# Sums of weight blocks by accumulating transfers in place of VectorE, with two signs turned and P4 last in each pair

## The chip, the core and the metric

The kernel runs on one core of a Trainium2 chip. The core has a matrix engine (TensorE, PE in the profile, with PEld for its weight loads), a vector engine (VectorE, DVE), an activation engine (ScalarE, ACT), a general engine (GpSimd, POOL) and a queue that only issues transfers (SyncE, SP). Each engine works through its own list of instructions in order, and waits for the others by semaphores. Transfers (DMAs) run beside the engines on 16 DMA engines that all queues share. The metric is the time of one execution on the device, in microseconds.

## The reference

One decoder block on 1024 tokens of width 1024, all in float32:

```
proj = x @ w_in                     # 1024 x 7168: q, f, i, og, pool_v, gate_a, gate_b
a = HGRN2(silu(q), f, i)            # 8 heads of 128, a gated recurrence in time
a = rmsnorm(a) * g * sigmoid(og) @ w_a
b = w_pool . (causal mean of pool_v over 2, 4, 8, 16 tokens - pool_v) * pool_scale
mix = (sigmoid(gate_a) * a + sigmoid(gate_b) * b) @ w_out
x = LN(alpha * x + mix)
x = LN(alpha * x + relu(x @ w_up)^2 @ w_down)
```

The products are most of the work: with w_in, w_a, w_out, w_up (1024 x 4096) and w_down (4096 x 1024).

## The kernel before

**Precision.** A float32 operand is split into a high part in the type that TensorE multiplies (a copy on ScalarE, `A.copy`, L118) and a low part, the rest (a subtraction on VectorE, L119). A product is then three matmuls, high x high, high x low and low x high.

**The half-size scheme.** All large products but the one with w_out use Strassen's scheme in the form that Winograd gave it: both operands are cut into 2 x 2 blocks, and seven products of half size replace eight. The activations' blocks (a11, a12, a22) and sums (s1 to s4) are made once per stage, split and kept (`xp`). The weights' sums are made anew for every pair of column blocks. A pair is two blocks of 128 columns, each cut into an upper and a lower half of the rows: b11 and b21 are the first block's halves, b12 and b22 the second's, each 128 partitions x 512 values (256 KB). Its seven products, each 12 matmuls of 128 x 128 by 128 x 512 (four row blocks, three matmuls each), are

| product | activation | weights | adds to |
|---|---|---|---|
| P1 | a11 | b11 | bank a |
| P2 | a12 | b21 | bank c |
| P7 | s3 | b22 - b12 (t3) | bank z |
| P6 | s2 | t3 + b11 (t2) | bank a |
| P4 | a22 | b21 - t2 (t4) | bank z |
| P5 | s1 | b12 - b11 (t1) | bank a |
| P3 | s4 | b22 | bank a |

A bank is a region of PSUM, the memory that TensorE writes. Between P1, P6, P5 and P3, which add onto the same bank, its running value is taken out: P1's and P6's by a copy on ScalarE (L271), P5's by an addition on VectorE (L275). P7's value is copied from bank z before P4 adds to it.

**`pair`** (L263) builds these steps: `t3`, `t2`, `t4`, `t1` make the weights' sums on VectorE (`w_diff`, L241; L284; L289) into a tile of the ring t (two buffers), and `w_part` splits a block or a sum into two tiles of the ring w (ten buffers, so five operands at a time). `p1` to `p7` are the products with what takes their results. With `twin=True` two pairs run interleaved and have an order of their own. `run` (L357) issues the steps of one pair, or of several together.

**Loads.** A pair's four blocks come by SP into two buffers of the ring raw: one holds b11 and b12, the other b21 and b22. For neighbouring column blocks a half is one transfer of 512 KB (L217), otherwise each block is one of 256 KB (L223).

**Stages.** (1) The values i of all heads, by rows of tokens. (2) The heads: for each of eight heads the pair of its q and f columns (`head_inputs`), and for two halves of the tokens the recurrence (`hgrn`), in which VectorE, ScalarE, GpSimd (small products of decays: T, eq and ek, L819 to L838) and TensorE take turns; between them stand the pairs of the output gates, of the pooling and, towards the end, of the gates (`gates`, `pool_products`). (3) The product with w_a, in twin pairs. (4) The product with w_out and the first norm. (5) The pairs of w_up: the first two as twins, the third with its blocks in other buffers, thirteen more alone (L1211), each followed by the sums of its squared ReLUs that the next stage needs. (6) w_down and the second norm.

**The order.** The kernel is written with a framework that plans the order on each engine from a simulated timeline: it takes the ready instruction that the program has first, changed by `high_priority` and `issue_after`. What the program writes pair after pair is therefore interleaved with neighbouring pairs and with the recurrence. In the program a pair's order is P1, P2, then P6 and P7, then P5 and P4, then P3. The order in which each queue then runs is fixed.

GpSimd issues eight transfers in this kernel (`load_y`, L1293, rows of the residual stream of 4 KB each); all others come from SP, and a few from ScalarE.

Of the kernel before, what the change touches and what calls it, by code (L numbers as in the profile page):

```python
# [43 lines left out]
def tile_hybrid_block(  # L44
# [126 lines left out]

    def first_tokens(name, *tags):
        for kp in range(CH):
            ps, _ = transposed(r[:CH], HALF if name == "a12" else 0, kp, tags[kp % len(tags)])
            in_parts(name, kp, ps)
            A.copy(xt[name == "a12"][kp], ps)

    def second_tokens(name, *tags):
        a11, a12, s = xt
        turned = []  # L180
        for kp in range(CH):
            if name in ("s3", "a22"):
                ps, done = transposed(r[CH:], HALF if name == "a22" else 0, kp, tags[kp % len(tags)])
                turned.append(done)
            if name == "s3":
                V.tensor_sub(s[kp], a11[kp], ps)
            elif name == "s1":
                V.tensor_add(a11[kp], s[kp], a11[kp])
            elif name == "s4":
                V.tensor_sub(a12[kp], a12[kp], s[kp])  # L190
            in_parts(name, kp, dict(s3=s, s2=s, s1=a11, s4=a12)[name][kp] if name != "a22" else ps)
            if name == "a22":
                V.tensor_sub(s[kp], ps, s[kp])
        return turned
# [44 lines left out]
    def w_diff(a, b):  # L239
        t = wq.tile([P, CH, P], F32, tag="t", name=nm("t"), bufs=2)  # L240
        V.tensor_sub(t, a, b)  # L241
        return t

# [19 lines left out]
    def pair(raw, rooms, takes, pz_tag="pj", twin=False, pc_tag="pj"):  # L263


        b11, b12, b21, b22 = raw if len(raw) == 4 else (raw[kh][:, :, n] for kh in range(2) for n in range(2))
# [11 lines left out]
        def t3():  # L278
            c["t"] = w_diff(b22, b12)
            return w_part(c["t"])  # L280

        def t2():
            if not twin:
                V.tensor_add(c["t"], c["t"], b11)  # L284
            return w_part(c["t"])

        def t4():
            if not twin:
                V.tensor_sub(c["t"], b21, c["t"])  # L289
                return w_part(c["t"])  # L290
            V.tensor_add(c["t"], c["t"], b11)
            V.tensor_sub(b21, b21, c["t"])
            return w_part(b21)

        def t1():
            return w_part(w_diff(b12, b11))
# [46 lines left out]
        def b_22():  # L343
# [8 lines left out]
                else (((t3, t2), ((t2, p6), (t3, p7))), ((t1, t4), ((t1, p5), (t4, p4))))  # L352
            ),
            ((b_22,), ((b_22, p3),)),
        )
# [46 lines left out]
    with tc.tile_pool(name="xr", bufs=8, side="right", reuse_waits="tile") as xr:  # L402
# [122 lines left out]
        def take_p5(c, ps):  # L525
            V.tensor_add(c22[c], c22[c], ps)
            put(1, 1, c, c22[c])

        def take_p3(c, ps):
            t = c_soon()  # L530
            A.copy(t, ps)
            put(0, 1, c, t)
# [9 lines left out]
        with behind_parts("a12"):  # L542
            for k in range(CH):
                V.tensor_sub(b22[k], b22[k], b12[k])
            w = parts(b22)
# [3 lines left out]
        with behind_parts("s3"):  # L549
            for k in range(CH):  # L550
                V.tensor_add(b22[k], b22[k], b11[k])
                V.tensor_sub(b21[k], b21[k], b22[k])
            w = parts(b21)
# [7 lines left out]
        with tc.issue_after(taken["a22", 1]):  # L561
            for k in range(CH):
                V.tensor_sub(b12[k], b12[k], b11[k])
            w = parts(b12)
# [40 lines left out]
    def o_sums(kp, tile_of=c_tile):  # L605

        a11, a21, a12, a22 = (loaded(od[k][u], tile_of) for k, u in ((kp, 0), (kp, 1), (kp + CH, 0), (kp + CH, 1)))
        V.tensor_add(a22, a21, a22)
        V.tensor_sub(a21, a11, a21)
        V.tensor_sub(a11, a22, a11)  # L610
        V.tensor_sub(a12, a12, a11)
        for name, t in zip(("s3", "s2", "s1", "s4"), (a21, a11, a22, a12)):
            nc.sync.dma_start(out=osd[name][kp], in_=t)
# [4 lines left out]
    with tc.tile_pool(name="tmp", bufs=1, side="right", reuse_waits="tile") as tmp:  # L618
# [24 lines left out]
        def head_inputs(h, behind=()):  # L643
# [6 lines left out]
            def take_f(u):  # L650
                def take(src):
                    t = fs[u] = fs[u] or tt("f")
                    A.activation(t, src, AF.Sigmoid)
                    A.activation(t, t, AF.Identity, bias=lb[:, h : h + 1], scale=one_lb[:, h : h + 1])
                return take

            def take_q(u):
# [7 lines left out]
                loaded_blocks(w_in, h * P, D + h * P), (c_soon, c_late, room_f),  # L665
# [8 lines left out]
        def output_gates(h):  # L674

            def take(dst, src=False):
                def put(t):
                    s = c_late() if src else t
                    A.activation(s, t, AF.Sigmoid)
                    nc.sync.dma_start(out=dst, in_=s)  # L680
                return put

            run(pair(
                loaded_blocks(w_in, 3 * D + h * P, 3 * D + (h + 1) * P), (c_soon, c_late, c_late),
                (take(ogd[h][0]), take(ogd[h + 1][0], True), take(ogd[h][1]), take(ogd[h + 1][1])),
            ))

        def gates(j):
# [3 lines left out]
            def take(dst, src=None, more=None):  # L692
                def put(t):
                    s = (tt("v") if spare else c_late()) if src else t
                    more_of = loaded(more, lambda: tt("v")) if more is not None else None
                    A.activation(s, t, AF.Sigmoid)
# [7 lines left out]
                loaded_blocks(w_in, 5 * D + j * P, 6 * D + j * P), rooms,  # L704
                (take(gad[j][0]), take(gbd[j][0], True, more[0]), take(gad[j][1]), take(gbd[j][1], False, more[1])),
# [26 lines left out]
        def pooled(g):  # L732
# [3 lines left out]
            def mean(c, u):  # L736

                for lo in (QUARTER, 0):
# [8 lines left out]
                    if u == 0 and lo == 0:  # L747
                        n += win - 1
                        V.tensor_mul(cur[:, HALO:n], cur[:, HALO:n], inv_n[:, : win - 1])
                        V.tensor_sub(pv[:, HALO:n], cur[:, HALO:n], pv[:, HALO:n])  # L750
                    V.scalar_tensor_tensor(pv[:, n:], cur[:, n:], 1.0 / win, pv[:, n:], ALU.mult, ALU.subtract)
# [11 lines left out]
            def first(c, i):  # L763
                G.memset(c[:, :HALO], 0.0)
                mean(c, 0)
                put(c, i, 0)

            def second(c, i):
                mean(c, 1)
# [12 lines left out]
            def take_12(ps):  # L782
# [7 lines left out]
                loaded_blocks(w_in, 4 * D + j * P, 4 * D + (j + 1) * P),  # L790
# [154 lines left out]
        nxt = head_inputs(0, (None, None, "p6", None, None))  # L945
# [40 lines left out]
        def gated(j, u, park):  # L986

            def take(src):
                t = loaded(gad[j][u], mg_tile("ga", 12))
                V.tensor_mul(t, t, src)  # L990
# [10 lines left out]
        def a_pair(p):  # L1001
            raw = loaded_blocks(w_a, 2 * p * P, (2 * p + 1) * P, raw_tile if p % 2 else mg_raw)
            room = mg_tile("room", 4)
            takes = [gated(2 * p + i, u, p < 2) for u in range(2) for i in range(2)]
# [131 lines left out]
    with tc.tile_pool(name="up", bufs=1, side="right", reuse_waits="tile") as up:  # L1136
# [10 lines left out]
        def relu2(t, src):  # L1147
            A.activation(t, src, AF.Relu)
# [3 lines left out]
        def units(i, raw):  # L1152
# [5 lines left out]
            def take(n):  # L1158
                def take(src):
                    h[n] = relu2(c_tile() if n == 1 else src, src)  # L1160
                return take

            def last(src):
                take(1)(src)
                h11, h12, h21, h22 = h
# [15 lines left out]
            return pair(raw, (c_tile,) * 3, (take(0), last, take(2), take(3)), "hg", i < 2, "tr" if i == 2 else "pj")  # L1181
# [29 lines left out]
        for i in range(3, NP):  # L1211
            raw, load = up_blocks(i)
            w_load = load(0, 1)
            if i == NP - 2:
                for part in down_rows(0, ws0):
                    part(w_load)
# [185 lines left out]
```

## Time and profile before

| | |
|---|---|
| median of 3 runs | 1461.77 us (1460.99 to 1465.17) |
| the profiled execution | 1460.19 us, span 1458.5 us |
| TensorE busy | 1436.4 us |
| VectorE busy | 1141.6 us |
| ScalarE busy | 758.3 us |
| GpSimd busy | 58.6 us |
| moved by DMA | 226.82 MB |

The profile is of one execution. The page gives the busy time of each engine, the same in 40 equal slices of the span with the clock that was granted to TensorE (PEclk) and the busy share of the DMA engines, then the chain of work that ended last, and groups of instructions by line. In a group, `out<-in` are the program's names, then the shapes, `xcount | busy, mean ns of one | idle time before them <- what ended it`. A row of waits reads: engine, what it wanted to write and its line, `<-` what it waited for: us in total, times, longest. A row of DMA issues ends with the size in KB and the median us from issue to landing. A row of stretches gives their length and, for each engine, busy us and the number of instructions, then the granted clock, the DMA share and GB/s. A timeline row is start, duration, engine, line, operation. `L118` is line 118.

### The profile page before, as it was taken

The page shows a single profiled execution, that of the slowest core. Times are in us where ns is not written, and L with a number is a line of the kernel's source. Part 1 is how long each engine was busy: PE and PEld are TensorE (multiplying, and loading weights), DVE is VectorE, ACT ScalarE, POOL GpSimd, SP SyncE. Part 2 cuts the span into 40 slices and gives each one's busy share as a digit, 9 for nine tenths or more (in the row PEclk, how much of TensorE's full clock was granted, in tenths as well). Part 3 has the DMA queues.
Part 4 walks back from the last instruction along what each step waited for, and adds up shares of the span by engine and source line. Part 5 has one row for each costly group of instructions (what it writes and reads, how often), then busy time and mean ns, then how long its engine had stood idle before and what let it go on. Part 6 is the DMA issues. An engine that isn't in the chain of part 4 may idle for free.

```text
span 1458.5 us, 20662 instructions
## 1 busy us (share of the span) xinstructions
PE 1436.4 (98%) x7377; PEld 1187.9 (81%) x7377; DVE 1141.6 (78%) x1838; ACT 758.3 (52%) x1383; POOL 58.6 (4%) x244
## 2 busy tenths in 40 slices
PE   8999999999999998999999999999999999999997
PEld 7888888888888886788888878888888888888886
DVE  5967989899898885768985597666666787777977
ACT  5445565666656655556542376555555443333535
POOL 0001001001000010000002100000000100000000
PEclk9999999999999999999999999999999999999999
DMA  7232233323234447897672225444474874445322
GB/s 253 70 126 87 85 98 101 109 75 114 90 99 138 152 132 249 301 299 241 223 247 99 73 94 195 159 146 144 152 261 149 275 260 150 153 141 163 130 73 116
DMA packets 160615, 226.82 MB, mean 156 GB/s; under 512 B 11232, under 2 KB 84480, under 8 KB 160512
## 3 DMA queue, kind: packets, MB, share of 16 engines
q1 hardware_dynamic: 158576, 218.93, 44.7%
q0 software_dynamic: 1152, 4.19, 0.8%
q10 hardware_dynamic: 784, 2.38, 0.5%
q8 instruction: 58, 0.95, 0.3%
q14 instruction: 45, 0.37, 0.1%
HBM read 154.16 MB, written 71.30 MB: 155 GB/s over the span
## 4 chain that ended last, share of the span: by engine, by line
PE 94%; DVE 3%; DMA 1%; ACT 1%; issue 0%; SPq 0%; DVEq 0%
PE ps_pj L201 16%; PE ps_pj L203 16%; PE ps_pj L204 16%; PE ps_pj L1283 4%; PE ps_pj L1285 4%; PE ps_pj L1284 4%; PE ps_pj L106 3%; PE ps_pj L107 3%; PE ps_pj L105 2%; PE ps_tr L1285 1%; PE ps_tr L1283 1%; PE ps_tr L1284 1%; PE ps_sc L201 1%; PE ps_sc L203 1%; PE ps_sc L204 1%; PE ps_hg L203 1%
## 5 line engine op out<-in xcount | busy, mean ns | idle before, releaser
L201 PE MATMUL ps_pj<-act,w 128*128 128x512 f32 x1068 | 421.6, 395 | 0.4 <-ACT act L123 0.2
L203 PE MATMUL ps_pj<-act,w 128*128 128x512 f32 x1068 | 415.1, 390 | 0.5 <-DVE act L124 0.5
L204 PE MATMUL ps_pj<-act,w 128*128 128x512 f32 x1068 | 414.1, 390 | 0.0
L201 PEld LDWEIGHTS ps_pj<-act,w 128*128 128x128 f32 x1068 | 200.6, 188 | 42.8 <-ACT act L123 0.6
L204 PEld LDWEIGHTS ps_pj<-act,w 128*128 128x128 f32 x1068 | 200.5, 188 | 42.3
L203 PEld LDWEIGHTS ps_pj<-act,w 128*128 128x128 f32 x1068 | 200.6, 188 | 40.6 <-DVE act L124 0.9
L118 ACT CAST w<-t 128x512 fp32r<-128x512 f32 x170 | 104.7, 620 | 105.0 <-PE ps_pj L203 53.8
L118 ACT CAST w<-raw 128x512 fp32r<-128x512 f32 x143 | 88.2, 620 | 117.3 <-PE ps_pj L203 62.5
L119 DVE TENSOR_TENSOR w<-raw,w 128x512 fp32r<-128x512 f32 x143 | 99.8, 702 | 55.2 <-ACT w L118 53.9
L119 DVE TENSOR_TENSOR w<-t,w 128x512 fp32r<-128x512 f32 x170 | 115.9, 685 | 29.6 <-ACT w L118 29.4
L1245 ACT CAST act<-act 128x1024 fp32r<-128x1024 f32 x66 | 66.9, 1050 | 107.9 <-issue 35.0
L1246 DVE TENSOR_TENSOR act<-act,act 128x1024 fp32r<-128x1024 f32 x66 | 79.3, 1220 | 18.5 <-ACT act L1245 15.8
L1285 PE MATMUL ps_pj<-act,act 128*128 128x512 f32 x240 | 92.9, 389 | 0.0
L1284 PE MATMUL ps_pj<-act,act 128*128 128x512 f32 x240 | 92.9, 389 | 0.0
L1283 PE MATMUL ps_pj<-act,act 128*128 128x512 f32 x240 | 92.4, 389 | 0.0
L275 DVE TENSOR_TENSOR c<-c,ps_pj 128x512 f32<-128x512 f32 x95 | 64.5, 681 | 18.0 <-PE ps_pj L204 13.4
L271 ACT COPY c<-ps_pj 128x512 f32<-128x512 f32 x96 | 55.2, 582 | 12.8 <-PE ps_pj L204 12.8
L817 DVE RECIPROCAL tC<-tA 128x128 f32<-128x128 f32 x64 | 54.1, 904 | 0.0
L1284 PEld LDWEIGHTS ps_pj<-act,act 128*128 128x128 f32 x240 | 45.1, 188 | 9.4
L1285 PEld LDWEIGHTS ps_pj<-act,act 128*128 128x128 f32 x240 | 45.1, 188 | 9.4
L1283 PEld LDWEIGHTS ps_pj<-act,act 128*128 128x128 f32 x240 | 45.1, 188 | 9.3
L241 DVE TENSOR_TENSOR t<-raw,raw 128x512 f32<-128x512 f32 x43 | 29.6, 689 | 21.9 <-DMA raw<-in_w_in_dram 19.7
(415 smaller groups left out, 2719.8 us busy)
## 6 DMA issues: line engine op xcount, KB each, us to landing
h<-c SPq DMA_DIRECT2D x106, 256.0 KB, 2.1
act<-h SPq DMA_DIRECT2D x78, 256.0 KB, 2.9
raw<-in_w_in_dram SPq DMA_DIRECT2D x64, 256.0 KB, 3.4
draw<-in_w_down_dram SPq DMA_DIRECT2D x16, 1024.0 KB, 7.8
raw<-in_w_up_dram SPq DMA_DIRECT2D x30, 512.0 KB, 4.2
raw<-in_w_in_dram SPq DMA_DIRECT2D x18, 512.0 KB, 4.0
hf<-h SPq DMA_DIRECT2D x34, 256.0 KB, 2.9
c<-o SPq DMA_DIRECT2D x24, 256.0 KB, 3.4
```

The source lines that it names most:

```text
L118: A.copy(hi, src)
L119: V.tensor_sub(lo, src, f(hi))
L201: PE.matmul(ps, wh[:, k], th, start=first and k == 0, stop=False, skip_group_check=True)
L203: PE.matmul(ps, wh[:, k], tl, start=False, stop=False, skip_group_check=True)
L204: PE.matmul(ps, wl[:, k], th, start=False, stop=k == CH - 1, skip_group_check=True)
L271: A.copy(t, ps)
L275: V.tensor_add(t, t, ps)
L1245: A.copy(hi, src)
L1246: V.tensor_sub(lo, src, f(hi))
L1283: PE.matmul(ps, hh[:, w], wh, start=fresh and n == 0, stop=False, skip_group_check=True)
L1284: PE.matmul(ps, hh[:, w], wl, start=False, stop=False, skip_group_check=True)
L1285: PE.matmul(ps, hl[:, w], wh, start=False, stop=n == M - 1, skip_group_check=True)
```

## The change

37 pairs (24 of w_in and thirteen of w_up) no longer make their weights' sums on VectorE. A class `SummedBlocks` loads b11, b21 and b22 as they are, b22 once more into a tile of the ring t and b11 once more into a place t1, all by SP, 256 KB each. Onto these GpSimd issues transfers that read another block from memory and add it to what stands in the tile (`accum_op=ALU.add`): b12 onto t (giving t3) and b12 onto t1 at once, b11 onto t once t3 has been split (t2), and b21 onto t once t2 has been split (t4). The two raw buffers of a pair now hold b11 with b21, and b22 with t1. b12 alone is not loaded any more.

Such a transfer can only add, so two signs of the scheme are turned until every sum of weight blocks is a plain sum: t3 is b22 + b12, t2 is t3 + b11, t4 is b21 + t2, t1 is b12 + b11. Sums of activations change their signs with it (`minus_sum`, one VectorE operation in place of another). The second column block's outputs come out negated; their users turn them back: a scale of -1 in the sigmoids, the ReLUs and a copy, a sign in the pooling's and the merge's VectorE operations.

The order in the program is P1, P2, P7, P6, P5, P3 and P4 last, one operand per step. In `units` the sums after the ReLUs are issued with whichever of the four results comes last.

The first stage, the w_a stage, the first three pairs of w_up and w_down keep their sums on VectorE. The prefetch of w_down's rows follows the last load of a pair as before.

```diff
+    def t_tile():
+        return wq.tile([P, CH, P], F32, tag="t", name=nm("t"), bufs=2)
+
+    def w_sum(a, b):
+        t = t_tile()
+        V.tensor_add(t, a, b)
         return t
+
+    class SummedBlocks:
+
+        def __init__(self, src, c1, c2, tile_of=raw_tile):
+            self.rows = src, (c1, c2)
+            (self.b11, self.b21), (self.b22, self.t1) = (
+                tile_of().rearrange("p k n c -> p (k n c)").rearrange("p (n k c) -> n p k c", n=2, c=P)
+                for _ in range(2)
+            )
+            self.t = t_tile()
+            self.load(self.b11, 0, 0)
+            self.load(self.b21, 1, 0)
+            self.load(self.t, 1, 1)
+            self.load(self.t1, 0, 0)
+            self.onto(self.t, 0, 1)
+            self.onto(self.t1, 0, 1)
+            self.last = self.load(self.b22, 1, 1)
+
+        def block(self, kh, n):
+            src, cols = self.rows
+            return src[kh * HALF : (kh + 1) * HALF, cols[n] : cols[n] + P].rearrange("(k p) c -> p k c", p=P)
+
+        def load(self, t, kh, n):
+            return nc.sync.dma_start(out=t, in_=self.block(kh, n))
+
+        def onto(self, t, kh, n):
+            nc.gpsimd.dma_start(out=t, in_=self.block(kh, n), accum_op=ALU.add)
...
         def t3():
-            c["t"] = w_diff(b22, b12)
+            c["t"] = w_sum(b22, b12) if b12 is not None else raw.t
             return w_part(c["t"])
 
         def t2():
-            if not twin:
+            if b12 is None:
+                raw.onto(c["t"], 0, 0)
+            elif not twin:
                 V.tensor_add(c["t"], c["t"], b11)
             return w_part(c["t"])
 
         def t4():
+            if b12 is None:
+                raw.onto(c["t"], 1, 0)
+                return w_part(c["t"])
...
         def t1():
-            return w_part(w_diff(b12, b11))
+            return w_part(w_sum(b12, b11) if b12 is not None else raw.t1)
...
-                else (((t3, t2), ((t2, p6), (t3, p7))), ((t1, t4), ((t1, p5), (t4, p4))))
+                else (((t3,), ((t3, p7),)), ((t2,), ((t2, p6),)), ((t1,), ((t1, p5),)))
             ),
             ((b_22,), ((b_22, p3),)),
+            *(() if twin else (((t4,), ((t4, p4),)),)),
         )
...
             run(pair(
-                loaded_blocks(w_in, h * P, D + h * P), (c_soon, c_late, room_f),
+                SummedBlocks(w_in, h * P, D + h * P), (c_soon, c_late, room_f),
                 (take_q(0), take_f(0), take_q(1), take_f(1)),
             ), behind=behind)
...
         for i in range(3, NP):
-            raw, load = up_blocks(i)
-            w_load = load(0, 1)
+            raw = SummedBlocks(w_up, i * 2 * P, i * 2 * P + P, up_raw_tile if i % 2 else raw_tile)
             if i == NP - 2:
                 for part in down_rows(0, ws0):
-                    part(w_load)
+                    part(raw.last)
             run(units(i, raw))
```

91 lines of the change are left out of this document (48 added, 43 removed).

## The prediction

> **What bounds the kernel now.** I read the page first: the busy shares, the chain that ended last, and the line of DMA shares by slice.
>
> ```profile
> PE 1436.4 (98%) x7377; PEld 1187.9 (81%) x7377; DVE 1141.6 (78%) x1838; ACT 758.3 (52%) x1383; POOL 58.6 (4%) x244
> ...
> DMA  7232233323234447897672225444474874445322
> ...
> PE 94%; DVE 3%; DMA 1%; ACT 1%; issue 0%; SPq 0%; DVEq 0%
> ```
>
> TensorE is busy 98% of 1458.5 us and carries 94% of the chain. A modelled busy share can hide small gaps, so I looked at the pitch of matmuls inside one product of the w_up stage (timeline, TensorE):
>
> ```profile
> 1041.20 0.39 PE L201 MATMUL ps_hg<-act,w 128*128 128x512 f32 x1
> ...
> 1043.69 0.39 PE L204 MATMUL ps_hg<-act,w 128*128 128x512 f32 x1
> 1043.92 0.39 PE L201 MATMUL ps_pj<-act,w 128*128 128x512 f32 x1
> ```
>
> Twelve matmuls take 2.72 us, 0.227 each, and the next product follows at that pitch: a pair of blocks (7 products) costs 7 x 2.72 = 19.0 us. The change leaves the number of matmuls alone, so it can only win what TensorE loses today. The waits of TensorE, and the stretches around the long one:
>
> ```profile
> PE ps_pj L105 <- ACT w L118: 4.7, 1, 4.7
> ...
> PE ps_hg L915 <- DVE st L883: 1.2, 1, 1.2
> PE ps_pj L106 <- DVE w L119: 0.8, 1, 0.8
> ```
>
> ```profile
> core 0: us, PE busy (x) PEld busy (x) DVE busy (x) ACT busy (x) POOL busy (x), PEclk, DMA share, GB/s
> ...
> 578.00:582.00 4.00, 0.19 (x2) 0.00 (x0) 2.00 (x4) 1.15 (x8) 0.00 (x0) 0.98 0.92 321
> 582.00:585.00 3.00, 2.11 (x5) 1.15 (x5) 1.37 (x4) 2.79 (x5) 0.00 (x0) 0.50 0.90 311
> 585.00:588.00 3.00, 3.00 (x8) 2.31 (x9) 0.64 (x1) 2.59 (x8) 0.00 (x0) 0.50 0.55 160
> ```
>
> One wait matters. At 578 us TensorE idles 4.7 us, and then the granted clock is 0.50 for the 6 us of the next two rows, a further 3.0 us lost: one long stall costs 7.7 us. It falls where the DMA share is 0.90 or more. The stages:
>
> ```profile
> 118.00:520.00 402.00, 401.76 (x2639) 333.53 (x2638) 358.71 (x701) 241.76 (x538) 32.36 (x176) 1.00 0.33 106
> 520.00:690.00 170.00, 163.10 (x838) 133.19 (x837) 124.42 (x210) 93.18 (x187) 4.21 (x20) 0.98 0.75 248
> ...
> 905.00:1150.00 245.00, 245.00 (x1083) 202.93 (x1082) 159.65 (x233) 139.51 (x231) 2.32 (x4) 1.00 0.51 176
> ```
>
> The heads (118 to 520) and w_up (905 to 1150) have TensorE filled to 0.24 us and to nothing; only the gates stage (520 to 690) has 6.9 us open. So a gain ends near 10 us, and a loss has no such end.
>
> **What goes.** Each of 37 pairs (24 of w_in, 13 of w_up) loses four sums on VectorE:
>
> ```profile
> L119 DVE TENSOR_TENSOR w<-t,w 128x512 fp32r<-128x512 f32 x170 | 115.9, 685 | 29.6 <-ACT w L118 29.4
> L118 ACT CAST w<-t 128x512 fp32r<-128x512 f32 x170 | 104.7, 620 | 105.0 <-PE ps_pj L203 53.8 <-DVE t L284 13.2 <-PE ps_hg L203 10.1
> ...
> L275 DVE TENSOR_TENSOR c<-c,ps_pj 128x512 f32<-128x512 f32 x95 | 64.5, 681 | 18.0 <-PE ps_pj L204 13.4 <-ACT c L271 2.1 <-issue 1.3
> L271 ACT COPY c<-ps_pj 128x512 f32<-128x512 f32 x96 | 55.2, 582 | 12.8 <-PE ps_pj L204 12.8
> L241 DVE TENSOR_TENSOR t<-raw,raw 128x512 f32<-128x512 f32 x43 | 29.6, 689 | 21.9 <-DMA raw<-in_w_in_dram 19.7 <-DMA raw<-in_w_a_dram 1.6
> ...
> L284 DVE TENSOR_TENSOR t<-t,raw 128x512 f32<-128x512 f32 x37 | 25.5, 688 | 0.7
> L289 DVE TENSOR_TENSOR t<-raw,t 128x512 f32<-128x512 f32 x37 | 25.4, 687 | 0.6
> ```
>
> 4 x 37 x 0.69 = 102 us of VectorE. TensorE waited 2.0 us on VectorE in the rows above, so I credit **-2 us**. The signs turned elsewhere swap an operation for one of the same shape, one for one: 0, on VectorE and ScalarE work that lies beside the matmuls and has more room than before.
>
> **What comes.** Per pair, 256 KB each: five loads on SP and four accumulating transfers on POOL's queue, 148 of the latter. The trace has no accumulating transfer. Nearest are loads of the same blocks and POOL's eight plain ones:
>
> ```profile
> raw<-in_w_in_dram SPq DMA_DIRECT2D x64, 256.0 KB, 3.4
> ...
> act<-x POOLq DMA_DIRECT2D x7, 512.0 KB, 6.7
> ```
>
> ```profile
> L1293 POOL DMA_DIRECT2D act<-x x7: 530/530/722, 1142.5 to 1152.7; - x7
> ...
> DMA to landing us min/median/max: 4.8/6.9/9.1
> ```
>
> I bound one from 4.8 to 9.1 us: the same queue, double the bytes, but rows of 4 KB and no addition. (Below 4.8 it is only better hidden.) Now three lie in a row on one tile: t is loaded, b12 added, split for P7; b11 added, split for P6; b21 added, split for P4. The old order shows how early an operand is ready (timeline: ScalarE's cast for P7, the sum that follows it, P7's first matmul, the copy of its result):
>
> ```profile
> 1024.85 0.62 ACT L118 CAST w<-t 128x512 fp32r<-128x512 f32 x1 [1.61 <-PE ps_pj L203]
> ...
> 1026.23 0.69 DVE L284 TENSOR_TENSOR t<-t,raw 128x512 f32<-128x512 f32 x1
> ...
> 1033.04 0.39 PE L201 MATMUL ps_hg<-act,w 128*128 128x512 f32 x1
> ...
> 1036.26 0.58 ACT L271 COPY c<-ps_hg 128x512 f32<-128x512 f32 x1
> ```
>
> The cast runs 8.2 us ahead of its product; a split is 0.62 + 0.69 = 1.31. P6 is due 8.2 + 2.72 = 10.9 us after that cast and has its operand after 1.31 + a + 1.31, so it is in time while a stays under 8.3. P4, put last, is due 8.2 + 4 x 2.72 = 19.1 us after it and needs three splits and two transfers, in time while their sum stays under 15.2. With a spread evenly over 4.8 to 9.1 the mean lateness is 0.8 x 0.8 / (2 x 4.3) = 0.07 us at P6, and for the sum of two 3.0^3 / (6 x 4.3^2) = 0.24 us at P4: 0.32 a pair, x 37 = **+12 us**. The ends are 0 and 37 x 3.0 = 111. The whole chain is 3.4 + 3a + 3.9 = 21.7 to 34.6 us a pair, which two t buffers (38 us) still carry.
>
> By the Trainium skill, "DMA: Bandwidth & Descriptors", section "Anatomy of one DMA", a transfer from GpSimd takes about 2.0 us and its bytes over 436 GB/s, 3.2 us for 512 KB and, as an estimate, 2.6 us for 256 KB; nothing would ever be late and the 12 us would go. The smallest landing quoted, 4.8 us, disagrees, so I do not sum by it. "TensorE: Matmul & The Clock Gate", Part 1, drops the clock after some 3.4 us idle; by that lateness of up to 3.0 us costs only itself, and the 0.50 behind the 4.7 us agrees as far as one case can.
>
> Some late operands are absorbed already:
>
> ```profile
> POOL T L819 <- DVE tA L811: 219.2, 15, 45.1
> ...
> POOL eq L830 <- DVE tA L863: 118.6, 14, 11.1
> ...
> POOL ek L835 <- DVE tC L865: 55.3, 13, 5.7
> ...
> DVE t L241 <- DMA raw<-in_w_in_dram: 19.7, 12, 3.5
> ...
> ACT w L118 <- DMA raw<-in_w_in_dram: 16.7, 8, 3.5
> ```
>
> Twenty such waits on loads, up to 3.5 us, are no wait of TensorE today; that holds the 12 us away from 111. A cast that waits for a late accumulation holds behind it on ScalarE the copies out of the banks (0.58 each, two to three a pair) and the activations, and TensorE may not add onto a bank before its copy; with a product of 2.72 us between, as today, a copy late by up to 2 us costs nothing, and beyond that it is the same lateness that the 12 and the 111 count.
>
> **Behind the waiting transfers on POOL** stand the recurrence's small operations, in three bunches (T, eq, ek) for each of 16 half-heads, 48 in all. A transfer costs POOL 0.53 us as shown, up to 2.1 if its cost goes with the four times as many row pieces. Some 19 pairs, 76 transfers, in the 402 us of the heads take 10 to 40% of POOL; a bunch meets one with that chance and waits half of it on average: 48 x (0.03 to 0.42) = 1 to 20 us on the recurrence. TensorE has other products to run meanwhile, so I let 4 us of it through, below the middle: **+4 us**. SP takes one to three more issues a pair, ahead of its stores:
>
> ```profile
> L217 SPq DMA_DIRECT2D raw<-in_w_up_dram x30: 367/383/393, 760.7 to 1094.3; - x30
> ```
>
> about 1 us in 19, hidden behind loads that may now start a pair earlier, since b11 and b21 share a buffer that is read out first; without that cover 37 us.
>
> **Traffic.** 9 blocks for 4: 1.3 MB more a pair. In w_up, 12 pairs in 245 us raise 176 GB/s to 240 and the share from 0.51 to 0.70. In the gates stage five pairs add 6.6 MB to 42 MB: 0.75 becomes 0.87 on average, in a stretch already at 0.9 and with the one long stall. I take one more such stall: **+8 us** (bounds -8, if the present one moves away, and +23, three more).
>
> **P4 last** leaves P6, P5 and P3 in a row on one bank, with a copy (0.58) or an addition (0.68) between. Uncovered it is 2 x 0.65 x 37 = 48 us; the planner puts products of the next pair between when it can, and I price it at 0.
>
> Sum: 1460.2 (the profiled execution's time; span 1458.5) - 2 + 12 + 4 + 8 = 1482.2. The median of the runs lies 1.6 us above that execution: **1484**.
>
> **Rivals.**
> *All hidden (0.20).* Accumulations land under 7 us and P4's place suffices: the terms vanish, 1460 to 1464. For it: the twenty absorbed waits. The fit of the Trainium skill's "DMA: Bandwidth & Descriptors", cited above, would lead here too. Against: three chained transfers a pair, with 1.4 us to spare at the median landing of 6.9 (10.9 - 2.62 - 6.9; 19.1 - 3.9 - 13.8).
> *The chain or the bank bounds the pair (0.25).* At 9.1 us each every P4 is 3.0 us late: 1462 + 111 = 1573 at the end, or the 48 us of the bank row: 1510. It decides from about 8 us a transfer.
> *Faster (0.10).* With 102 us off VectorE and another order in the gates stage, the stall at 578 us goes: 4.7 + 3.0 + 2.0 = 9.7, so 1452. It decides if the split named in that wait is ready within 4 us of the matmul before it. Against: that wait stands beside a DMA share of 0.92, which rises.
> *The planner does not put P4 last,* ordering by its own ready times: same prices, part of the second rival.
>
> **Numbers.** Forecast case 0.45, its own range 1467 to 1505. Leaving out most of the faster case below and the far half of the second above, 8 in 10 lie in 1456 to 1545. Within 0.3% (4.4 us) a measurement of this kernel can hardly tell a change; faster 0.10, same 0.20, slower 0.70.
>
> **What would show it.** VectorE's busy time falls by about 100 us. POOL's queue lists 148 transfers, with the true landing and issue time in their rows. TensorE's waits gain rows ending at ScalarE's or VectorE's split, behind DMA t. PEclk drops below 1 in more places between 520 and 690. The forecast is wrong if accumulations land under 5 us (then 1462) or over 9 (then past 1545).

## The result, and the profile after

| | before | after |
|---|---|---|
| median | 1461.67 us (1460.99 to 1465.17) | 1551.08 us (1549.63 to 1553.93) |
| the profiled execution | 1460.19 us, span 1458.5 us | 1550.59 us, span 1548.9 us |
| ratio after / before | | 1.0609, 95% interval 1.0586 to 1.0632 |

The change costs 89 us, where 22 were forecast; the time lies 6 us above the upper end of the forecast's range.

The page after: the busy shares, the DMA shares by slice, the line of the accumulating queue (packets, MB, share of 16 engines' span) and the chain that ended last.

```profile
PE 1467.6 (95%) x7377; PEld 1195.3 (77%) x7377; DVE 1050.3 (68%) x1690; ACT 746.4 (48%) x1383; POOL 245.3 (16%) x392
...
DMA  8356667668667778997764138889889694535322
...
q0 software_dynamic: 79296, 43.00, 21.2%
...
PE 21%; DMA 2%; DVE 1%; issue 0%; ACT 0%; POOL 0%; DVEq 0%; POOLq 0%; ACTq 0%
```

VectorE is 91.3 us less busy (1141.6 to 1050.3), as foreseen, and nothing is gained by it. The matmuls are the same 7377. The chain that ended last is followed without a gap only through the last stage, so its shares do not locate the loss; the waits of TensorE do.

```profile
PE ps_pj L204 <- ACT w L118: 24.8, 14, 7.4
PE ps_pj L204 <- ACT c L307: 10.6, 8, 4.0
PE ps_pj L204 <- DVE c L311: 6.9, 7, 1.5
PE ps_tr L976 <- ACT tH L973: 5.5, 5, 2.4
PE ps_hg L960 <- DVE st L928: 4.7, 3, 2.7
```

Before, one wait of 4.7 us mattered. Now TensorE waits for splits (ACT w), for copies out of a bank (ACT c), for additions out of a bank (DVE c) and for the recurrence. Behind them stand these waits of the other engines:

```profile
POOL t L275 <- DVE w L119: 309.3, 58, 20.2
DVE w L119 <- ACT w L118: 267.8, 123, 10.9
ACT w L118 <- DMA t<-in_w_in_dram: 128.0, 38, 7.0
ACT w L118 <- DMA t<-in_w_up_dram: 80.5, 25, 6.3
```

ScalarE stands 63 times, 208.5 us in all, at the cast of a sum that has not landed; VectorE waits for ScalarE, and GpSimd's next addition waits for VectorE. The transfers themselves, from the rows of the line that issues them (duration of the issue: least, median and most in ns, then when the first and the last began; the last row is from issue to landing in us, for all transfers of the line):

```profile
L275 POOL DMA_DIRECT2D t<-in_w_in_dram x72: 1258/1282/1853, 29.3 to 709.7; - x72
L275 POOL DMA_DIRECT2D t<-in_w_up_dram x39: 1282/1282/1854, 947.1 to 1219.7; - x39
...
DMA to landing us min/median/max: 4.2/5.6/13.4
```

The stretches after that answer to those before (heads, gates, w_up), and the longest stall, which stands in w_up (the DMA share sums the times of packets, so it can pass 1):

```profile
120.00:545.00 425.00, 407.63 (x2632) 335.30 (x2632) 318.47 (x629) 236.67 (x536) 117.74 (x245) 0.99 0.70 150
545.00:735.00 190.00, 166.97 (x816) 131.45 (x815) 109.28 (x183) 90.88 (x184) 28.26 (x39) 0.96 0.87 243
941.00:1225.00 284.00, 262.11 (x1109) 208.29 (x1108) 125.53 (x194) 136.13 (x240) 64.48 (x50) 0.98 0.88 211
1174.00:1182.00 8.00, 0.56 (x3) 0.22 (x2) 0.24 (x1) 1.48 (x3) 0.00 (x0) 0.69 1.19 295
1182.00:1189.00 7.00, 6.33 (x17) 4.42 (x18) 2.48 (x5) 3.13 (x7) 1.30 (x1) 0.62 1.01 285
```

Since the stretches do not hold quite the same matmuls, I compare the time per matmul. Heads: 425/2632 against 402/2639, 24 us more over 2632. Gates: 190/816 against 170/838, 24 us more. W_up: 284/1109 against 245/1083, 33 us more. The loss is spread over all stages that use the new sums. The DMA share of w_up is 0.88, not the 0.70 forecast. The long stall of the gates is still there, as TensorE's timeline shows, and the one of 7.4 us in w_up has come on top:

```profile
580.60 0.79 PE L204 MATMUL ps_pj<-act,w 128*128 128x512 f32 x1 [3.98 <-ACT c L307]
```

What one such loss looks like, in a w_up pair without a long stall (timeline; in brackets the idle time before and what ended it), first ScalarE:

```profile
1054.27 0.62 ACT L118 CAST w<-t 128x512 fp32r<-128x512 f32 x1 [1.34 <-PE ps_pj L206]
1057.94 0.63 ACT L1193 ACTIVATE c<-c 128x512 f32<-128x512 f32 x1 [3.04 <-DVE c L311]
1064.18 0.62 ACT L118 CAST w<-t 128x512 fp32r<-128x512 f32 x1 [5.61 <-DMA t<-in_w_up_dram]
```

VectorE in the same stretch:

```profile
1054.92 0.69 DVE L119 TENSOR_TENSOR w<-t,w 128x512 fp32r<-128x512 f32 x1 [1.67 <-ACT w L118]
...
1064.83 0.69 DVE L119 TENSOR_TENSOR w<-t,w 128x512 fp32r<-128x512 f32 x1 [6.93 <-ACT w L118]
1065.44 0.68 DVE L311 TENSOR_TENSOR c<-c,ps_pj 128x512 f32<-128x512 f32 x1
```

TensorE, the first matmul behind the gap:

```profile
1066.17 0.50 PE L204 MATMUL ps_pj<-act,w 128*128 128x512 f32 x1 [0.84 <-DVE c L311]
```

And GpSimd, two issues in a row:

```profile
1056.71 2.60 POOL L275 DMA_DIRECT2D t<-in_w_up_dram  x2 [2.14 <-DMA t<-in_w_up_dram]
```

ScalarE casts t3 at 1054.27, reaches the cast of t2 at 1058.57, 4.3 us later, and stands there 5.6 us until the addition has landed. VectorE stands 6.9 us at the split's second half, and behind it waits an addition that takes a finished product out of a bank. TensorE may not add the next product onto that bank before, and stops. The late operand here is not the sum, but what was queued behind it.

GpSimd's row shows one reason why the sum is so late. The split of t3 ends at 1055.6, but the first of the two issues, which the landing of a plain load of t has released, is a first sum of a later pair; t2's transfer stands behind it in GpSimd's queue. By the row of the tile t from 1058 us on it begins at 1057.5, 1.9 us after the split; it lands 6.6 us later. In ten of the thirteen pairs of w_up the two are issued back to back like this.

```profile
L275 POOL DMA_DIRECT2D t<-in_w_up_dram x2: 1282/1564/1847, 1057.5 to 1065.8; - x2
```

### The profile page after: what moved, and what is told of

It reads as the page before. It is cut to its first block, busy times and chain, and to the rows that moved or that the text cites. A ratio compares the mean times of both kernels' runs of the same rounds, so it can differ in the third digit from the quotient of the medians.

```text
span 1548.9 us, 21124 instructions
## 1 busy us (share of the span) xinstructions
PE 1467.6 (95%) x7377; PEld 1195.3 (77%) x7377; DVE 1050.3 (68%) x1690; ACT 746.4 (48%) x1383; POOL 245.3 (16%) x392
## 3 DMA queue, kind: packets, MB, share of 16 engines
q0 software_dynamic: 79296, 43.00, 21.2%
## 5 line engine op out<-in xcount | busy, mean ns | idle before, releaser
L204 PE MATMUL ps_pj<-act,w 128*128 128x512 f32 x1068 | 430.2, 404 | 44.9 <-ACT w L118 24.8
L207 PE MATMUL ps_pj<-act,w 128*128 128x512 f32 x1068 | 419.1, 396 | 3.0 <-DVE w L119 2.8
L206 PE MATMUL ps_pj<-act,w 128*128 128x512 f32 x1068 | 420.1, 395 | 0.5 <-DVE act L124 0.5
L204 PEld LDWEIGHTS ps_pj<-act,w 128*128 128x128 f32 x1068 | 203.6, 191 | 101.7 <-ACT w L118 31.8
L119 DVE TENSOR_TENSOR w<-t,w 128x512 fp32r<-128x512 f32 x133 | 91.7, 689 | 225.6 <-ACT w L118 225.6
L207 PEld LDWEIGHTS ps_pj<-act,w 128*128 128x128 f32 x1068 | 203.4, 190 | 51.7 <-DVE w L119 8.3
L206 PEld LDWEIGHTS ps_pj<-act,w 128*128 128x128 f32 x1068 | 203.9, 191 | 41.0 <-DVE act L124 0.9
L118 ACT CAST w<-t 128x512 fp32r<-128x512 f32 x133 | 82.5, 620 | 275.0 <-DMA t<-in_w_in_dram 128.0
L119 DVE TENSOR_TENSOR w<-raw,w 128x512 fp32r<-128x512 f32 x180 | 124.7, 697 | 29.1 <-ACT w L118 26.5
L275 POOL DMA_DIRECT2D t<-in_w_in_dram x72 | 93.2, 1302 | 290.2 <-DVE w L119 193.8
L118 ACT CAST w<-raw 128x512 fp32r<-128x512 f32 x180 | 109.4, 615 | 29.1 <-PE ps_pj L206 7.4
L275 POOL DMA_DIRECT2D t<-in_w_up_dram x39 | 50.3, 1419 | 135.6 <-DVE w L119 115.5
L275 POOL DMA_DIRECT2D raw<-in_w_in_dram x24 | 30.8, 1282 | 184.1 <-DMA raw<-in_w_in_dram 47.9
L1328 PEld LDWEIGHTS ps_pj<-act,act 128*128 128x128 f32 x240 | 45.0, 188 | 9.4
```

The source lines that it names most:

```text
L118: A.copy(hi, src)
L119: V.tensor_sub(lo, src, f(hi))
L204: PE.matmul(ps, wh[:, k], th, start=first and k == 0, stop=False, skip_group_check=True)
L206: PE.matmul(ps, wh[:, k], tl, start=False, stop=False, skip_group_check=True)
L207: PE.matmul(ps, wl[:, k], th, start=False, stop=k == CH - 1, skip_group_check=True)
L275: nc.gpsimd.dma_start(out=t, in_=self.block(kh, n), accum_op=ALU.add)
```

## The experiments

Three theories stood at the start. *Held queues*: ScalarE and VectorE, in order, stand at sums that have not landed, and what is queued behind them is late. *Load*: the transfers delay all others, whoever waits. *Order*: P6, P5 and P3 in a row on one bank cost the time.

**The new order and signs, all sums on VectorE** (the other w_in pairs are edited like the first).

```diff
-                SummedBlocks(w_in, h * P, D + h * P), (c_soon, c_late, room_f),
+                loaded_blocks(w_in, h * P, D + h * P), (c_soon, c_late, room_f),
...
-            raw = SummedBlocks(w_up, i * 2 * P, i * 2 * P + P, up_raw_tile if i % 2 else raw_tile)
+            raw, load = up_blocks(i)
+            w_load = load(0, 1)
...
```

> The changed kernel with its signs and its order (P4 last), but with the 37 pairs' sums back on VectorE from blocks loaded as before. Held queues (ScalarE and VectorE, in order, wait for the landings of the chained sums, and what stands behind them is late): no such waits are left, 1456 to 1468 us. Load (the transfers themselves, on POOL and the DMA engines): none left either, the same. Order (P6, P5 and P3 in a row on one bank): nothing of it is undone, 1510 to 1550 us.

Measured: 1468.89 us, ratio 1.0037 (1.0025 to 1.0050). *Order* falls as the main cause: order and signs together cost 0.4%.

**Only the first sums (t3, t1) by transfers.**

```diff
-                raw.onto(c["t"], 0, 0)
+                V.tensor_add(c["t"], c["t"], b11)
...
-                raw.onto(c["t"], 1, 0)
+                V.tensor_add(c["t"], c["t"], b21)
```

> Of the four sums of a pair only t3 and t1, which wait for no split, stay accumulating transfers; t2 and t4 are VectorE additions again. Held queues: in the changed kernel the first sum had landed 12 to 40 us ahead of its cast, so nothing is held, 1456 to 1470 us. Load: half the accumulating transfers and all five loads remain, about 1505 us. Order: 1510 to 1550 us.

Measured: 1469.77 us, 1.0042 (1.0027 to 1.0057): no more than the kernel before it. Two accumulating transfers a pair, which wait for no split, are free, and *Load*, which gave 1505, missed here.

**Only the chained sums (t2, t4) by transfers.**

```diff
...
-            self.load(self.t, 1, 1)
-            self.load(self.t1, 0, 0)
-            self.onto(self.t, 0, 1)
-            self.onto(self.t1, 0, 1)
+            self.load(self.b12, 0, 1)
...
-            c["t"] = w_sum(b22, b12) if b12 is not None else raw.t
+            c["t"] = w_sum(b22, b12 if b12 is not None else raw.b12)
...
```

> The other half: t3 and t1 are VectorE additions from blocks loaded once, t2 and t4 stay accumulating transfers behind the splits. Held queues: both held waits of a pair remain, 1530 to 1555 us. Load: half the accumulating transfers and one load less, about 1505 us. Order: 1510 to 1550 us.

Measured: 1527.84 us, 1.0443 (1.0425 to 1.0461). The same number of accumulating transfers as in the run above, with one load less a pair, costs 58 us more when they stand between splits. The number alone is not the cause.

**The same traffic, the two additional landings waited for by no split.** The chained sums are on VectorE, and after the last split two additions more land on the tile, which nothing reads.

```diff
-                raw.onto(c["t"], 0, 0)
+                V.tensor_add(c["t"], c["t"], b11)
...
+                V.tensor_add(c["t"], c["t"], b21)
+                w = w_part(c["t"])
+                raw.onto(c["t"], 0, 0)
                 raw.onto(c["t"], 1, 0)
-                return w_part(c["t"])
+                return w
```

> As the kernel with only t3 and t1 summed by transfers, and after the split of t4 two more accumulating transfers are issued onto the tile t, which nobody reads any more: the full traffic of the changed kernel, with GpSimd waiting for splits as there, and no ScalarE or VectorE instruction waiting for these two landings. Held queues: within 15 us of the kernel without the two. Load: back to 1535 to 1555 us.

Measured: 1503.86 us, 1.0275 (1.0258 to 1.0291), 2.3% or 34 us over the first sums alone. That is between what the two theories gave, so *Load* has a share. The run is not pure: the tile is given back later, GpSimd waits for that, and in w_up ScalarE stands 65.0 us at first sums that land later for it. The granted clock is 0.984 here and 0.996 with the first sums alone, so up to 18 of the 34 us are lost clock behind a few long waits.

```profile
POOL t L275 <- DMA t<-in_w_in_dram: 251.9, 46, 26.7
...
ACT w L118 <- DMA t<-in_w_up_dram: 65.0, 11, 8.9
```

**The old order of the steps with all sums by transfers.**

```diff
-                else (((t3,), ((t3, p7),)), ((t2,), ((t2, p6),)), ((t1,), ((t1, p5),)))
+                else (((t3, t2), ((t2, p6), (t3, p7))), ((t1, t4), ((t1, p5), (t4, p4))))
...
-            *(() if twin else (((t4,), ((t4, p4),)),)),
...
```

> The changed kernel with all its accumulating transfers, but with the order of steps before (P6 with P7, P5 with P4, P3 last). Held queues: t4 is asked for earlier behind the same two landings, so more is held, 1555 to 1600 us. Order (P6, P5 and P3 in a row are what makes late copies and additions cost TensorE time): better than the changed kernel, 1515 to 1540 us.

Measured: 1596.58 us, 1.0920 (1.0904 to 1.0936), as *Held queues* gave; *Order* had it faster than the changed kernel. In the old order t2 follows t3 at once. P4 last, with one operand per step, is worth 45 us within this scheme.

**Transfers that overwrite.** Everything as in the changed kernel, down to the order of the instructions on each engine, but the transfers do not add, so the kernel leaves the sums out.

```diff
-            nc.gpsimd.dma_start(out=t, in_=self.block(kh, n), accum_op=ALU.add)
+            nc.gpsimd.dma_start(out=t, in_=self.block(kh, n))
```

> The changed kernel with the four transfers of each pair as plain ones that overwrite (so the sums are left out and the weights are wrong); issue, waits and order are the same. Per engine 32 pieces go at 27 ns, not 65, so a landing is 1.2 us earlier, 2 x 37 x 1.2 = 89 us of the 208 us that ScalarE waits for landings. Held queues: the loss shrinks in that proportion, 1500 to 1525 us. If the length of the wait does not matter: 1545 to 1555 us.

Measured: 1476.51 us, 1.0099 (1.0081 to 1.0116), far below what either theory gave. Its queue on the page:

```profile
q0 software_dynamic: 12992, 43.00, 9.8%
```

Its waits of ScalarE for sums:

```profile
ACT w L118 <- DMA t<-in_w_in_dram: 63.3, 32, 4.5
...
ACT w L118 <- DMA t<-in_w_up_dram: 30.2, 17, 4.5
```

And the issues with their landings:

```profile
L275 POOL DMA_DIRECT2D t<-in_w_up_dram x39: 747/747/756, 902.8 to 1146.2; - x39
...
DMA to landing us min/median/max: 3.2/4.0/8.2
```

The bytes are the same 43.00 MB, but in 12992 packets for 79296 and at 9.8% of the DMA engines for 21.2%; a transfer lands in 4.0 us for 5.6 and is issued in 0.75 for 1.28. The wait of ScalarE falls from 208.5 to 93.5 us. (The 43.00 MB are the 148 transfers and eight plain ones of the rows of the residual stream.) Chains, extra loads and order stay and cost 1.0%. So 5.1 of the 6.1%, some 75 us, belong to what adding costs over writing. The run does not separate the longer landing from the longer issue and the busier DMA engines.

**t2 later in the program.** The splits of t1 and b22 are written ahead of t2's.

```diff
-                else (((t3,), ((t3, p7),)), ((t2,), ((t2, p6),)), ((t1,), ((t1, p5),)))
+                else (((t3,), ((t3, p7),)), ((t1, b_22, t2), ((t2, p6), (t1, p5), (b_22, p3))), ((t4,), ((t4, p4),)))
...
```

> The changed kernel with the splits of t1 and b22 written ahead of that of t2, so that ScalarE has two more casts to do while t2's transfer lands; order of products, transfers and traffic as in the changed kernel. Held queues: one of the two held waits of a pair shrinks by up to 2.5 us, 1505 to 1535 us. Load: no change, 1545 to 1555 us.

Measured: 1604.04 us, 1.0963 (1.0918 to 1.1008), the wrong way. ScalarE's waits for sums fell little (208.5 to 200.0 us: 137.6 and 62.4), while TensorE's waits for splits rose from 24.8 to 43.2:

```profile
PE ps_pj L204 <- ACT w L118: 43.2, 21, 4.2
```

*Held queues*, as it stood, would have gained here. A split moved back in the queue also moves t2, and with it t4's transfer; that this made the loss is likely, not shown.

**Accumulating transfers in w_up alone** (again all w_in pairs alike).

```diff
-                SummedBlocks(w_in, h * P, D + h * P), (c_soon, c_late, room_f),
+                loaded_blocks(w_in, h * P, D + h * P), (c_soon, c_late, room_f),
...
```

> Accumulating transfers only in the thirteen pairs of w_up; the 24 of w_in sum on VectorE, with the changed order. The stages are independent: the kernel with all sums on VectorE (1469 us) plus the 33 us that the w_up stage lost in the changed kernel, 1495 to 1508 us. If the loss before w_up were carried into it by another alignment of the queues: below 1485 us.

Measured: 1505.14 us, 1.0284 (1.0260 to 1.0308), 36 us over the kernel with all sums on VectorE. The stage alone shows about what it lost in the changed kernel (33 us by the stretches), so w_up's loss does not hang on what went before.

**Later splits.** Same transfers; t2's split is queued behind the copy of P1's value, t4's behind that of P6's.

```diff
-            A.copy(t, ps)
+            copies.append(A.copy(t, ps).ins)
...
+                with tc.issue_after(copies[0]):
+                    return w_part(c["t"])
...
-                return w_part(c["t"])
+                with tc.issue_after(copies[-1]):
+                    return w_part(c["t"])
```

> The changed kernel with the same transfers, in which the split of t2 is put on ScalarE behind the copy of P1's value, and the split of t4 behind the copy of P6's value (where they stood, ScalarE reached them before their transfers had landed, with copies and activations of the pair before queued behind them). Held queues: what the wait cost beyond the traffic goes, and the time falls towards that of the kernel with the idle accumulations, 1500 to 1525. Load: the transfers are the same, so the time stays at 1540 to 1560. Late operand: the chain is stretched further and P6 or P4 comes later, 1560 to 1600.

Measured: 1545.05 us, 1.0560 (1.0537 to 1.0584). ScalarE's waits for sums fell to 127.6 us, and the time by only 6. The loss came back elsewhere, as TensorE's waits show:

```profile
PE ps_pj L204 <- ACT c L307: 40.3, 26, 6.9
...
PE ps_pj L204 <- ACT w L118: 8.8, 6, 2.8
```

In its timeline, ScalarE's cast of t2 and the copy behind it:

```profile
1061.63 0.62 ACT L118 CAST w<-t 128x512 fp32r<-128x512 f32 x1 [5.99 <-DMA t<-in_w_up_dram]
...
1067.02 0.59 ACT L307 COPY c<-ps_pj 128x512 f32<-128x512 f32 x1
```

And the gap of TensorE that ends with this copy:

```profile
1067.66 0.50 PE L204 MATMUL ps_pj<-act,w 128*128 128x512 f32 x1 [1.98 <-ACT c L307]
```

The cast of t2 still comes 6 us too soon, now with the copies of the next products behind it. GpSimd issues t2's transfer behind a later pair's first sum here too. So I formed a fourth theory, *Chain*: t3's split, an addition, t2's split, an addition and t4's split follow each other in a loop, and the order leaves them too little time, wherever ScalarE waits.

**GpSimd freed of the recurrence.** T, eq, ek and the products they are made of run on VectorE, each edited like the first.

```diff
-            G.tensor_copy(T, blk(fd)[:, :, SUB - 1])
+            V.tensor_copy(T, blk(fd)[:, :, SUB - 1])
...
```

> The changed kernel with the recurrence's small operations of GpSimd (T, eq, ek) moved to VectorE, so that GpSimd issues transfers and little else. If the recurrence lost its time behind GpSimd's waiting transfers, the stretch up to the last recurrence shortens by most of the 48 us that it grew, 1505 to 1520. Held queues and Load both say that GpSimd's queue is not where it was lost: 1545 to 1560, with some us either way for the operations that VectorE takes on.

Measured: 1546.20 us, 1.0578 (1.0558 to 1.0599). The interval overlaps that of the changed kernel: that the recurrence stands behind transfers on GpSimd cost little, 0.3 points, not clear of noise. What the transfers cost each other on that queue this run does not touch.

**The first sums by transfers, in the old order.** The second kernel's edit and the old steps together.

> The kernel with the first sums by transfers and the chained ones on VectorE, but with the steps of a pair in the order of before (P6 and P7 together, then P5 and P4, then P3). Order: the three products in a row on one bank cost the 0.4% by which the sums on VectorE in the new order were slower, so this gives 1462 to 1466, the time of before. Held queues and Load: two transfers a pair that wait for no split cost nothing, the same 1462 to 1466. If the first sums cost something by themselves, 1468 to 1475.

Measured: 1461.56 us, 0.9995 (0.9983 to 1.0007), the time of before. VectorE has 1095.8 us of work for 1141.6. The 0.4% belong to the order, and 46 us off VectorE are worth nothing. No kernel here beats the one before.

**The chain spread out.** The later splits, and t3 split first of its pair's blocks.

```diff
...
         def t0():
+            if b12 is None:
+                c["t"] = raw.t
+                c["w3"] = w_part(raw.t)
             return w_part(b11)
```

> The kernel with the later splits (t2's behind the copy of P1's value, t4's behind the copy of P6's), and t3 now split first of its pair's blocks, ahead of b11's, so that some 11 us of products lie between t3's split and t2's, and 8 us between t2's and t4's, where the transfers in between take about 8 and 6 with their issue. Same transfers, same products. Chain (two landings in a row that the order left too little time for, wherever ScalarE waits for them): the waits of TensorE go, and what stays is the traffic, as with the idle accumulations: 1500 to 1520. Load: 1540 to 1560, as the kernel changed and the one with the later splits.

Measured: 1515.85 us, 1.0383 (1.0355 to 1.0411), in the range of *Chain*: 1.8 points, 26 us, under the later splits alone, with the same transfers. ScalarE hardly waits for sums any more, 33.6 us for 208.5, while the DMA share of w_up is no lower, 0.91. ScalarE's and TensorE's waits:

```profile
ACT w L118 <- DMA t<-in_w_up_dram: 16.9, 5, 6.6
ACT w L118 <- DMA t<-in_w_in_dram: 16.7, 7, 5.2
...
PE ps_pj L204 <- ACT c L307: 18.4, 23, 1.9
PE ps_pj L204 <- ACT w L118: 8.4, 2, 5.7
```

The stretch of its w_up stage:

```profile
941.00:1189.00 248.00, 235.21 (x1012) 190.37 (x1011) 112.36 (x172) 126.48 (x218) 59.51 (x47) 0.99 0.91 214
```

In ScalarE's queue the casts of sums now stand some 10 us apart, with no idle time before them (a row of two holds the last cast of one pair and the first of the next):

```profile
1074.03 0.62 ACT L118 CAST w<-t 128x512 fp32r<-128x512 f32 x1
...
1084.00 1.14 ACT L118 CAST w<-t 128x512 fp32r<-128x512 f32 x2
```

But the run changes more than this spacing. On GpSimd, t2's transfer now follows the split of t3 at once, and the first sum that a load releases comes behind it:

```profile
1086.24 1.28 POOL L275 DMA_DIRECT2D t<-in_w_up_dram  x1 [2.35 <-DVE w L119]
1089.21 1.28 POOL L275 DMA_DIRECT2D t<-in_w_up_dram  x1 [1.69 <-DMA t<-in_w_up_dram]
```

Which of the two brought the 26 us is not shown. 18.4 us of what is left are TensorE's waits for copies; that my placing of the splits delays them is likely, not shown.

**The runs by stage.** All traces have the same 7377 matmuls, so the time from one matmul to another of the same numbers can be compared stage by stage. Each row is one profiled execution, in us:

| kernel | heads (2632 matmuls) | gates (816) | w_up (1109) |
|---|---|---|---|
| before | 401 | 165 | 251 |
| changed | 425 | 190 | 285 |
| all sums on VectorE, new order | 402 | 173 | 252 |
| first sums only | 404 | 167 | 251 |
| chained sums only | 430 | 193 | 258 |
| first sums and unread additions | 404 | 190 | 267 |
| transfers that overwrite | 402 | 174 | 255 |
| later splits | 424 | 190 | 287 |
| chain spread out | 413 | 179 | 275 |

The rows of heads and w_up, of the chained sums alone and then of the unread additions:

```profile
120.00:550.00 430.00, 409.50 (x2635) 338.85 (x2634) 338.74 (x665) 238.65 (x537) 73.07 (x211) 0.98 0.48 118
...
950.00:1208.00 258.00, 254.58 (x1111) 208.79 (x1110) 143.96 (x220) 138.40 (x240) 33.41 (x26) 0.99 0.71 194
```

```profile
115.00:519.00 404.00, 403.75 (x2634) 334.30 (x2633) 339.68 (x664) 242.17 (x538) 138.22 (x248) 1.00 0.75 161
...
915.00:1182.00 267.00, 256.67 (x1112) 210.66 (x1111) 143.06 (x220) 137.03 (x240) 62.16 (x49) 0.98 0.91 221
```

The stages lose by different causes. In the heads the chained sums alone cost all of the loss, at a DMA share of 0.48, and the unread additions cost 3 us at 0.75: there it is the chain. In the gates either one brings as much as both. In w_up the chained sums alone cost 7 us and the unread additions 15, for 33 in the changed kernel, more than the two: there the losses do not simply add. With the chained sums alone, GpSimd has no first sum to issue ahead of t2's transfer, and the transfers of w_up land in a median of 4.5 us, for 5.9 in the changed kernel; which of these matters no run separates. The chain spread out gives back 12, 11 and 10 us, and w_up still loses 24 although ScalarE waits there only 16.9 us for sums.

## Why the prediction was wrong

**The late operands (+12 us) are the step that failed.** Its mechanism was right, two transfers in a row between splits, and the bound of one transfer from issue to landing, 4.8 to 9.1 us, holds the measured median of 5.6, though the extremes are 4.2 and 13.4. The size was not: the chained sums alone cost 58 us over the first sums alone, where the step gave 12 and 111 as its end. Three assumptions made it small:

- *The slack of the old order.* The 8.2 us were read from a cast to its product, and P6 counted as in time while a transfer stays under 8.3. But ScalarE waits where the cast stands in its queue: in the pair shown it has reached the cast of t2 4.3 us after that of t3, and in 37 pairs it met a sum that had not landed 63 times. With the casts some 10 us apart the waits fell to 33.6 us, and 2.3 of the 6.1%, 33 us, came back, in part perhaps by the order on GpSimd.
- *The transfer began at its split.* GpSimd's queue was priced for the recurrence only; for the chain it was put at nothing. In the pair shown 1.9 us pass there before the issue, and 6.6 after it: 8.5 us from split to landing, over the 8.3, with a landing inside the range. No run varies this order alone.
- *What is queued behind.* "A copy late by up to 2 us costs nothing, and beyond that it is the same lateness" counted a pair's late operand once. The timeline shows one late sum holding ScalarE for 5.6 us and VectorE for 6.9, with the addition out of another bank behind them. Neither that lateness nor the twenty absorbed waits of up to 3.5 us bounded it.

**Traffic (+8 us) was sized by bytes.** The bytes came as said, but an accumulating queue that moves 43.00 MB takes 21.2% of the DMA engines where a plain one takes 9.8%, so w_up stood at 0.88 for the 0.70 forecast (the gates stage at 0.87, as forecast). The run with unread additions puts the traffic's price at up to 34 us; by stage it is 23 us in the gates and 15 in w_up over the first sums alone, and nothing in the heads. One more long stall came, as assumed, but in w_up, beside a DMA share of 1.19, and it costs half clock as well; that of the gates stayed. Over the whole span the granted clock falls from 0.996 to 0.985:

```profile
core 0: 1548.9 us, clock 0.985
```

0.015 x 1548.9 = 23 us of lost clock for 0.004 x 1458.5 = 6 before: up to 17 of the 89 us are paid for having waited, not in the waiting.

**The rest held.** VectorE's relief (-2) was 91 us of busy time and worth nothing, as the first sums alone in the old order show. The recurrence behind GpSimd's transfers (+4): an issue of 1.28 us lies between the 0.53 and 2.1 I gave, and taking the recurrence off GpSimd moved the time by 3 in 1000, inside the intervals. That the transfers wait for each other there was not in the sum. P4 last (0) costs 0.4% by itself, some 6 us of the 48 that the row of the bank would cost uncovered, and within the scheme it gains 45.

**The rivals.** The one that happened is the second, "the chain or the bank bounds the pair": 1551 lies between its 1510 and 1573. I gave it 0.25 and let it decide from about 8 us a transfer; it decided at a median landing of 5.6, which the way from split to landing made 8.5 in the pair shown. "All hidden" would have needed the chain to have its time.

**The cited rules.** The Trainium skill, "DMA: Bandwidth & Descriptors", "Anatomy of one DMA", gave an estimate of 2.6 us for 256 KB. Every landing of these transfers is longer, 4.2 us at least with addition and 3.2 without. The Trainium skill's "TensorE: Matmul & The Clock Gate", Part 1, was read as a price for idle stretches above 3.4 us only; here some shorter waits cost half clock too. TensorE's timeline in the changed kernel:

```profile
967.88 0.50 PE L204 MATMUL ps_sc<-act,w 128*128 128x512 f32 x1 [2.60 <-ACT w L118]
```

The stretch that follows:

```profile
968.80:972.20 3.40, 3.40 (x9) 2.62 (x9) 1.65 (x3) 1.66 (x4) 1.09 (x1) 0.50 0.85 222
```

A wait of 2.60 us is followed by 3.4 us at 0.50, which cost 1.7 us more. The longest waits of the rows `ps_tr L976` and `ps_hg L960` above, 2.4 and 2.7 us, are followed by no such step, so no threshold can be read from this. The measurement decides: lateness of up to 3.0 us did not always cost only itself.

**What stays open.** How the 75 us of adding divide between longer landings, longer issues and busier DMA engines; how much of the loss in w_up is GpSimd's order of transfers; why in the gates either cause alone costs as much as both. The 34 us for unread traffic and the 33 us got back by the last run were not measured on the same kernel.

## What to carry to other kernels

Before putting a transfer between two instructions of an in-order engine, ask where in that engine's queue its landing is waited for, and what stands ahead of it on the queue that issues it; whether the last operand is in time for its product does not settle it. Two accumulations a pair with nothing ahead of them were free, two between splits cost 58 us. Moving the wait in the queue gained 6 us; splitting the first link earlier as well, 33 in all. Look at such a loss stage by stage: two transfers a pair between splits cost 28 us in the heads and 7 in w_up. Freeing an engine that is not the bound, 91 us of VectorE here, is no gain to set against that.

## What the runs showed of the hardware

- The queue of the accumulating transfers moved its 43.00 MB in six times as many packets as with plain ones (79296 against 12992) and took 2.3 times the DMA engines' time (21.2% of 1548.9 us against 9.8% of 1475.4). One transfer of 256 KB took 1.28 us of GpSimd for 0.75 and a median of 5.6 us to land for 4.0.
- A TensorE wait of 2.60 us was followed by one step of 3.4 us at half clock, one of 2.7 us was not.
